# A router kernel on one core: spare matrix products while TensorE waits, a written-out first trip, an early table load, and one load fewer

## The chip, the cores and the metric

The kernel runs on one core of a Trainium2 chip. The metric is the device time in microseconds; the kernel before takes 85.81 us (median of three runs, 85.59 to 85.82). The profiled execution has a span of 84.4 us, from its first to its last instruction.

## The reference

```python
def setup_inputs():
    batch, seq, dim = 16, 512, 1024
    num_loras = 8
    return {
        "x": np.random.randn(batch, seq, dim).astype(np.float32),
        "router_weights": np.random.randn(dim, num_loras).astype(np.float32),
    }

def reference(x, router_weights):
    logits = np.matmul(x, router_weights)
    exp_logits = np.exp(logits - np.max(logits, axis=-1, keepdims=True))
    return (exp_logits / np.sum(exp_logits, axis=-1, keepdims=True)).astype(np.float32)
```

There are 8192 rows of x, each of 1024 numbers. Every row is multiplied by a 1024 x 8 matrix and a softmax is taken over the 8 results. The input x is 33.55 MB, the output 0.26 MB.

## The kernel before

Each of the 128 partitions holds 64 rows of x (the text calls them rows 0 to 63; one such "row" is 128 rows of the input, one a partition). Rows 0 to 3 are loaded as float32 from the Sync queue and cast by ScalarE. Rows 4 to 63 are loaded by GpSimd's queue, which turns float32 into bfloat16 on the way. TensorE transposes the eight 128 x 128 blocks of a row, VectorE copies five of them from PSUM to SBUF and ScalarE three, and TensorE multiplies the copies with the weights. Groups of eight rows then go through the softmax on VectorE and ScalarE.

```python
LOADS = [4] + [8] * 4 + [4] * 4 + [2, 2, 2] + [1] * 5   # rows in each load
PIECES = [4, 2, 2]                     # row 63 comes in three pieces of its columns
G, SKIP = 8, 4
TRIPS = 31
VN, SN = 5, 3                          # blocks copied by VectorE, by ScalarE
# ... (cut)
X_AT = place[0]
xa = sb("x_all", [P, J, D], bf16)      # all 64 rows have their own place: no load waits for a buffer
x_f32 = sb("x_f32", [P, LOADS[0], D], fp32)
# ... (cut)  Sync tells TensorE of rows as their loads land
for i, r in enumerate(LOADS):
    if i:
        sp.wait_ge(s_ld[i], 16)
        sp.sem_inc(s_in, r)
# ... (cut)  the loads, all issued at the start on one queue
for i, r in enumerate(LOADS):
    if i:
        nc.gpsimd.dma_start(
            out=xa[:, first[i]:first[i] + r, :], in_=x_rows[:, first[i]:first[i] + r, :]
        ).then_inc(s_ld[i], 16)
# ... (cut)
def loop_turn(b):                      # transposes one row; its address is in registers r_x
    pe.wait_ge(s_in, 1).then_inc(s_in, -1)
    for c in range(KO):
        t = again(turn_like, ...)      # eight transposes 128x128
    # ... (cut) registers go on by one row

def multiply(b, dst):
    for c in range(KO):
        if c == 0:
            pe.wait_ge(s_c[b], 2).then_inc(s_c[b], -2)
        m = ...                        # eight products 128x8

def fill():                            # a spare product; its result is never read
    return pe.matmul(spare, lhsT=filler[:, 0:P], rhs=filler, start=True, stop=True)
# ... (cut)
turn(0)
pe.wait_ge(s_wb, 1)
nc.br("rows_turn", engines=only_pe)
with nc.body("rows_multiply", valid_engines=only_pe):
    fill()
    fill()
    multiply(1, None)
    pe.br("rows_turn")
with nc.body("rows_turn", valid_engines=only_pe):
    loop_turn(1)
    multiply(0, None)
    loop_turn(0)
    pe.br_lt(r_x[0], left_of(TRIPS - 1), on_true="rows_multiply", on_false="rows_done")
nc.switch_bb("rows_done")
# ... (cut)  after the loop: row 63 by its pieces
pe.wait_ge(s_c[(J - 3) % 2], 2)
turn_piece(0)
multiply((J - 3) % 2, alone[1])
turn_piece(1)
turn_piece(2)
multiply((J - 2) % 2, alone[2])
# ... (cut)  ScalarE's start
act.wait_ge(s_f, 16).then_inc(s_f, -16)   # rows 0 to 3 have landed
for i in range(2):
    cast(i)
    for j in (2 * i, 2 * i + 1):
        act_copy(j, j)
```

Of the kernel before, what the change touches and what calls it, by code (L numbers as in the profile page):

```python
# [11 lines left out]
def kernel(  # L12
# [6 lines left out]
    nc = tc.nc  # L19
    P = 128  # L20
    B, S, D = x.shape
# [10 lines left out]
    fp32 = mybir.dt.float32  # L32
    bf16 = mybir.dt.bfloat16
    Exp = mybir.ActivationFunctionType.Exp
    X = mybir.AxisListType.X
    ALU = mybir.AluOpType

    LOADS = [4] + [8] * 4 + [4] * 4 + [2, 2, 2] + [1] * 5  # L40
    PIECES = [4, 2, 2]
    G, SKIP = 8, 4
    TRIPS = 31
# [5 lines left out]
    DONE = ends[-1]  # L49
    assert sum(LOADS) == J - 1 and sum(PIECES) == KO and ends[-1] == J - ALONE  # L50
    VN, SN = 5, 3

    place = [16640]

    def sb(name, shape, dtype):
        size = mybir.dt.size(dtype)
        for n in shape[1:]:
            size *= n
        at = place[0]
        place[0] = -(-(at + size) // 64) * 64  # L60
        return nc.alloc_sbuf_tensor_at(name, shape, dtype, offset=at).ap()
# [1 line left out]
    def ps(name, shape, dtype):  # L63
        return nc.alloc_psum_tensor(name, shape, dtype).ap()

    X_AT = place[0]
    xa = sb("x_all", [P, J, D], bf16)
    x_f32 = sb("x_f32", [P, LOADS[0], D], fp32)
    identity = sb("identity", [P, P], bf16)
    ident = sb("ident", [P, P], fp32)  # L70
    w8 = sb("w8", [KO, P, N], fp32)
# [31 lines left out]
    s_w = nc.alloc_semaphore("s_w")  # L103
    s_ld = [sem(f"s_ld{i}") for i in range(len(LOADS))]
    s_z = [sem(f"s_z{i}") for i in range(len(PIECES))]
# [21 lines left out]

    first = [sum(LOADS[:i]) for i in range(len(LOADS))]
    cols = [sum(PIECES[:i]) for i in range(len(PIECES))]


    with tc.manual_schedule():
        early = [
            nc.sync.dma_start(out=x_f32, in_=x_rows[:, 0:LOADS[0], :]).then_inc(s_f, 16),
            nc.scalar.dma_start(
# [25 lines left out]

    for j in range(LOADS[0]):
        sp.wait_ge(s_cast, j + 1)
# [34 lines left out]
    pe = nc.tensor  # L198
    r_x = [pe.alloc_register(f"rx{c}") for c in range(KO)]
    r_l = pe.alloc_register("rl")  # L200
    for c, r in enumerate(r_x):

        pe.reg_mov(r, X_AT + D * 2 + c * P * 2 + (P - 1) * 2)
    pe.reg_mov(r_l, LG_AT + 256 * (SKIP - 1))

    def at(ap, like, r):
        return mybir.RegisterAccessPattern(
            ap=ap, dtype=like.dtype, memsetref=like.tensor.name + "_set",
            regref=r.name, is_regloc_offset=False, reg_ap_offset=r.name,
            const_ap_offset=0, const_sub_tensor_id=0,  # L210
        )

    def again(like, **k):
        return pe.add_instruction(copy.replace(like, name=f"I-{nc.next_id()}", **k))

    def turn_ap(b, c):
        return (ptv if c < VN else pts)[b][:, c if c < VN else c - VN, :]

    def chunk(b, c):
        return xTv[b][:, c, :] if c < VN else xTs[b][:, c - VN, :]  # L220

    def loop_turn(b):

        pe.wait_ge(s_in, 1).then_inc(s_in, -1)  # L224
        for c in range(KO):
            t = again(
                turn_like,
                ins=(turn_like.ins[0], at([[J * D, P], [1, P]], xa, r_x[c])),
                outs=(pe.lower_ap(turn_ap(b, c), opt=False),),
            )  # L230
            if c == VN - 1:
                t.then_inc(s_tv, 1)
            if c == KO - 1:
                t.then_inc(s_ts, 1)
        pe.reg_add(r_l, r_l, 256)
        for c in range(KO):
            if c == KO // 2:
                pe.reg_alu(r_l, r_l, -4097, ALU.bitwise_and)
            pe.reg_add(r_x[c], r_x[c], D * 2)
# [10 lines left out]
# [5 lines that stand above are left out]
            if dst is None:  # L255
                m = again(
                    mult_like,
                    ins=(
                        pe.lower_ap(w_bf[:, c, :], opt=False),
                        pe.lower_ap(chunk(b, c), opt=False, for_matmul_weights=True),  # L260
                    ),
                    outs=(at([[2 * G * 64, P], [1, N]], lg, r_l),),
                    start_tensor_calc=(c == 0),
                    stop_tensor_calc=(c == KO - 1),
                )
            else:
                m = pe.matmul(  # L267
                    dst, lhsT=chunk(b, c), rhs=w_bf[:, c, :],
                    start=(c == 0), stop=(c == KO - 1),
                )  # L270
            if c == KO - 1:
                m.then_inc(s_p, 1)

    def fill():
        return pe.matmul(spare, lhsT=filler[:, 0:P], rhs=filler, start=True, stop=True)  # L275
# [17 lines left out]
    def left_of(i):  # L293

        return X_AT + D * 2 * (2 * i + 3) + (P - 1) * 2

    only_pe = OrderedEngineSet([pe.engine])
    nc.br("rows_turn", engines=only_pe)
    with nc.body("rows_multiply", valid_engines=only_pe):
        fill()  # L300
        fill()
        multiply(1, None)
        pe.br("rows_turn")
    with nc.body("rows_turn", valid_engines=only_pe):
        loop_turn(1)
        multiply(0, None)
        loop_turn(0)
        pe.br_lt(r_x[0], left_of(TRIPS - 1), on_true="rows_multiply", on_false="rows_done")
    nc.switch_bb("rows_done")


# [30 lines left out]
    act = nc.scalar  # L342
# [14 lines left out]
    def act_copy(j, seen):  # L357

        act.wait_ge(s_ts, seen + 1)
        act.copy(xTs[j % 2], pts[j % 2][:, 0:SN, :]).then_inc(s_c[j % 2], 1)  # L360

    act.wait_ge(s_f, 16).then_inc(s_f, -16)  # L362
    for i in range(2):
        cast(i)
# [181 lines left out]
```

## Time and profile before

| Quantity | Value |
|---|---|
| Time, median of 3 runs | 85.81 us (85.59 to 85.82) |
| Span of the profiled execution | 84.4 us |
| Busy: TensorE products, TensorE weight loads | 62.4 us (74%), 52.3 us (62%) |
| Busy: VectorE, ScalarE, GpSimd | 39.4 us (47%), 38.0 us (45%), 11.3 us (13%) |
| Transposes of rows (L288) | 311 of 226 ns and 186 of 228 ns, as recorded |
| Spare products (L275, 128x512) | 61, 402 ns each as recorded |
| Table load of ScalarE | 1, 1.28 us, at 8.50 us |
| Read from HBM | 33.59 MB |

The engines are PE (TensorE's products), PEld (its weight loads), DVE (VectorE), ACT (ScalarE), POOL (GpSimd) and SP (Sync). L288 means line 288 of the kernel. A matrix product's recorded duration overlaps the next one's, so the step from one start to the next is what the engine really spends. A wait is listed with the engine that waits, the one that ended it, the total, the count and the longest. "PEq" is TensorE's own sequencer: a wait that ends there is one that the sequencer sat through, for a semaphore that was raised elsewhere.

### The profile page before, as it was taken

How to read it: one execution, taken by the hardware profiler on the slowest of the kernel's cores; microseconds unless marked ns; L12 is line 12 of the kernel's file. 1: busy time of each engine (PE TensorE's matmuls, PEld its weight loads, DVE VectorE, ACT ScalarE, POOL GpSimd, SP SyncE). 2: the span in 40 equal slices, each digit the busy share in tenths (PEclk: the TensorE clock that was granted, in tenths of full speed). 3: DMA queues.
4: the chain of work that ended last, by engine and by line, in shares of the span. 5: the costliest groups of instructions: out<-in, count | busy, mean ns of one | idle time of the engine just before them, and what ended most of it. 6: DMA issues, size and time to landing. Idle time of an engine off the chain costs nothing. (4 is left out here: it accounts for less than half of the span.)

```text
span 84.4 us, 2916 instructions
## 1 busy us (share of the span) xinstructions
PE 62.4 (74%) x1094; PEld 52.3 (62%) x1094; DVE 39.4 (47%) x114; ACT 38.0 (45%) x81; POOL 11.3 (13%) x26
## 2 busy tenths in 40 slices
PE   0070073999991999259990999999998799999870
PEld 0040072788871778238870688887887588777650
DVE  0030022247660685227660265678568357656662
ACT  0000988535460465225460254566546246546470
POOL 0699996000000000000000000000000000000000
PEclk9999999999999999999998579999999999999997
DMA  5999979997999799989998999999999999999930
GB/s 142 433 419 264 225 163 233 241 217 171 241 241 217 163 248 233 202 186 248 233 202 179 225 210 217 217 206 225 206 229 190 214 212 215 204 207 213 171 114 12
DMA packets 3184, 18.12 MB, mean 215 GB/s; under 512 B 488, under 2 KB 1000, under 8 KB 2032
## 3 DMA queue, kind: packets, MB, share of 16 engines
q0 software_dynamic: 2736, 15.73, 90.3%
q1 hardware_dynamic: 432, 2.36, 7.3%
q10 hardware_dynamic: 16, 0.03, 0.2%
HBM read 33.59 MB, written 0.26 MB: 401 GB/s over the span
## 5 line engine op out<-in xcount | busy, mean ns | idle before, releaser
L405 DVE COPY xTv<-ptv 128x640 bf16<-128x640 bf16 x63 | 31.0, 492 | 32.9 <-PE ptv L288 26.7
L360 ACT COPY xTs<-pts 128x384 bf16<-128x384 bf16 x63 | 30.1, 477 | 34.0 <-PE pts L288 33.6
L288 PE MATMUL ptv<-identity,x_all 128*128 128x128 bf16 x311 | 29.0, 226 | 14.4 <-PEq L224 9.5
L288 PEld LDWEIGHTS ptv<-identity,x_all 128*128 (+1 forms) x311 | 19.0, 99 | 15.4 <-issue 15.4
L288 PE MATMUL pts<-identity,x_all 128*128 128x128 bf16 x186 | 21.7, 228 | 0.0
L275 PEld LDWEIGHTS lg<-w_bf,xTv 128*128 128x128 bf16 x305 | 15.7, 98 | 7.9 <-issue 1.3
L275 PE MATMUL spare<-filler 128*128 128x512 bf16 x61 | 19.6, 402 | 0.2
L275 PE MATMUL lg<-w_bf,xTv 128*128 128x8 bf16 x305 | 16.7, 167 | 0.0
L288 PEld LDWEIGHTS pts<-identity,x_all 128*128 x186 | 13.9, 103 | 0.0
L275 PE MATMUL lg<-w_bf,xTs 128*128 128x8 bf16 x183 | 13.2, 166 | 0.0
L275 PEld LDWEIGHTS lg<-w_bf,xTs 128*128 128x128 bf16 x183 | 9.0, 96 | 0.0
L180 POOL DMA_DIRECT2D x_all<-in_x_dram x16 | 8.6, 588 | 2.2 <-POOLq L142 2.2
L275 PEld LDWEIGHTS spare<-filler 128*128 128x128 bf16 x61 | 4.7, 103 | 1.1 <-issue 1.0
L346 ACT ACT_TABLE_LOAD x1 | 1.3, 1283 | 8.5 <-ACTq L362 8.5
L282 PE MATMUL lg<-ident,w 8*128 8x8 f32 x8 | 1.0, 251 | 4.7 <-PEq L280 4.7
L346 ACT CAST x_all<-x_f 128x1024 bf16<-128x1024 f32 x4 | 4.0, 1044 | 0.0
L425 DVE TENSOR_REDUCE mx<-lg 128x8 f32 x8 | 1.8, 225 | 4.6 <-DVEq L475 4.1
L282 PEld LDWEIGHTS lg<-ident,w 8*128 8x128 f32 x8 | 0.9, 197 | 4.7 <-issue 4.7
L349 ACT ACTIVATE ev<-ex 128x64 f32<-128x64 f32 x8 | 2.1, 257 | 1.5 <-DVE ex L425 0.9
L396 DVE CAST identity<-ident 128x128 bf16<-128x128 f32 x1 | 0.5, 518 | 4.6 <-POOL ident L186 4.6
L441 DVE TENSOR_REDUCE ssum<-ev 128x8 f32<-128x64 f32 x8 | 1.7, 218 | 0.1
L425 DVE TENSOR_TENSOR ex<-lg,mx 128x64 f32<-128x64 f32 x8 | 1.7, 216 | 0.0
(41 smaller groups left out, 16.0 us busy)
## 6 DMA issues: line engine op xcount, KB each, us to landing
x_all<-in_x_dram POOLq DMA_DIRECT2D x4, 2048.0 KB, 27.7
x_all<-in_x_dram POOLq DMA_DIRECT2D x4, 1024.0 KB, 51.7
x_f<-in_x_dram SPq DMA_DIRECT2D x1, 2048.0 KB, 8.4
x_all<-in_x_dram POOLq DMA_DIRECT2D x3, 512.0 KB, 62.0
x_all<-in_x_dram POOLq DMA_DIRECT2D x5, 256.0 KB, 66.2
out_dram<-out_all SPq DMA_DIRECT2D x1, 240.0 KB, 2.0
x_all<-in_x_dram POOLq DMA_DIRECT2D x1, 128.0 KB, 67.8
x_all<-in_x_dram POOLq DMA_DIRECT2D x2, 64.0 KB, 67.5
```

What stands on the lines that cost most here:

```text
L180: nc.gpsimd.dma_start(out=xa[:, first[i]:first[i] + r, :], in_=x_rows[:, first[i]:first[i] + r, :]).then_inc(s_ld[i], 16)
L275: return pe.matmul(spare, lhsT=filler[:, 0:P], rhs=filler, start=True, stop=True)
L282: t = pe.transpose(w_ps[:, n, :], w8[:, :, n], ident[0:KO, 0:KO])
L288: turn_like = pe.transpose(turn_ap(0, 0), xa[:, 0, 0:P], identity).ins
L346: act.copy(xa[:, k, :], x_f32[:, k, :]).then_inc(s_cast, 1)
L349: return act.activation(ev, ex, func=Exp).then_inc(s_ev, 1)
L360: act.copy(xTs[j % 2], pts[j % 2][:, 0:SN, :]).then_inc(s_c[j % 2], 1)
L396: dve.tensor_copy(out=identity, in_=ident).then_inc(s_idb, 1)
L405: dve.tensor_copy(out=xTv[j % 2], in_=ptv[j % 2][:, 0:VN, :]).then_inc(s_c[j % 2], 1)
L425: return dve.add_instruction(kind(name=f"I-{nc.next_id()}", engine=dve.engine, **k))
L441: dve.reduce_sum(ssum[:, :, 0], ev, axis=X).then_inc(s_d, 1)
```

## The change

There are four parts.

1. A block of six spare products is put ahead of TensorE's loop. The loop goes through it before the rows that open a new load of eight (and before row 36), so that TensorE has something to do while it waits. A test of the row's address decides; for that test x is moved in SBUF to byte 40,960 of a partition (20 rows of 2 KB), and the float32 buffer is put ahead of it.
2. The loop's first trip is written out, so that the loop begins with the spare products and the multiplication of an odd row.
3. ScalarE loads its table of functions before it waits for rows 0 to 3, and no longer after.
4. Rows 52 to 62 come in seven loads, 3, 2, 2, 1, 1, 1, 1, where there were eight, 2, 2, 2, 1, 1, 1, 1, 1.

```diff
-    LOADS = [4] + [8] * 4 + [4] * 4 + [2, 2, 2] + [1] * 5
+    LOADS = [4] + [8] * 4 + [4] * 4 + [3, 2, 2] + [1] * 4
@@
+    LOT, SPARE = 8, 6
+    ROW_AT = 32 - LOADS[0] - LOT
+    assert LOADS[1:5] == [LOT] * 4 and 64 - ROW_AT == LOADS[0] + LOT * 5
@@
-    X_AT = place[0]
+    x_f32 = sb("x_f32", [P, LOADS[0], D], fp32)
+    place[0] = X_AT = ROW_AT * D * 2
     xa = sb("x_all", [P, J, D], bf16)
-    x_f32 = sb("x_f32", [P, LOADS[0], D], fp32)
@@
+    r_t = pe.alloc_register("rt")
@@
-    nc.br("rows_turn", engines=only_pe)
-    with nc.body("rows_multiply", valid_engines=only_pe):
+
+    loop_turn(1)
+    multiply(0, None)
+    loop_turn(0)
+    nc.br("rows", engines=only_pe)
+    with nc.body("rows_spare", valid_engines=only_pe):
+        for _ in range(SPARE):
+            fill()
+        pe.br("rows_even")
+    with nc.body("rows", valid_engines=only_pe):
         fill()
         fill()
         multiply(1, None)
-        pe.br("rows_turn")
-    with nc.body("rows_turn", valid_engines=only_pe):
         loop_turn(1)
         multiply(0, None)
+        pe.reg_alu(r_t, r_x[0], (64 + 32 + LOT - 1) * D * 2, ALU.bitwise_and)
+        pe.br_eq(r_t, 32 * D * 2, on_true="rows_spare", on_false="rows_even")
+    with nc.body("rows_even", valid_engines=only_pe):
         loop_turn(0)
-        pe.br_lt(r_x[0], left_of(TRIPS - 1), on_true="rows_multiply", on_false="rows_done")
+        pe.br_lt(r_x[0], left_of(TRIPS - 1), on_true="rows", on_false="rows_done")
     nc.switch_bb("rows_done")
@@
+    act.preload_act_table(Exp)
     act.wait_ge(s_f, 16).then_inc(s_f, -16)
```

## The prediction

> **What bounds the kernel now.** I read the DMA lines of the page first, then the waits of the Sync queue, then TensorE's timeline around its waits, then the chain that ended last.
>
> ```profile
> DMA  5999979997999799989998999999999999999930
> q0 software_dynamic: 2736, 15.73, 90.3%
> HBM read 33.59 MB, written 0.26 MB: 401 GB/s over the span
> ```
>
> The DMA engines are busy from the second slice to the 38th, so to about 80 us. GpSimd's queue alone fills 90.3% of their span. The input's 33.55 MB pass through them once and nothing else of size does.
>
> ```profile
> SPq L168 <- DMA x_all<-in_x_dram: 63.6, 16, 9.7
> ```
>
> Sync tells TensorE of each landed load, and it sits idle for all 16 loads in turn, 9.7 us for one of eight rows: 8 x 0.524 MB = 4.19 MB in 9.7 us is 432 GB/s. That is the pace at which rows come: 1.21 us each.
>
> ```profile
> 43.92 0.22 PE L275 MATMUL lg<-w_bf,xTs 128*128 128x8 bf16 x3
> 46.55 0.69 PE L288 MATMUL ptv<-identity,x_all 128*128 128x128 bf16 x5 [2.41 <-PEq L224]
> 47.04 0.52 PE L288 MATMUL pts<-identity,x_all 128*128 128x128 bf16 x3
> 47.36 1.06 PE L275 MATMUL spare<-filler 128*128 128x512 bf16 x2
> ...
> 64.99 0.22 PE L275 MATMUL lg<-w_bf,xTs 128*128 128x8 bf16 x3
> 66.02 0.44 PE L288 MATMUL ptv<-identity,x_all 128*128 128x128 bf16 x5 [0.81 <-PEq L224]
> ```
>
> TensorE (start, recorded duration, idle before in brackets) finishes row 27, waits 2.41 us for the load of rows 28 to 35, and then runs at half speed: five transposes are recorded with 0.69 us, where they have 0.44 later. It is at full speed again from row 30 (49.53 us). In spite of that it has caught up at row 48, where it waits 0.81 us again for a load. At full speed two rows with their two spare products take 1.73 us (start of the spare pair at 22.00, of the next at 23.73), 0.86 us a row against the 1.21 us in which rows come.
>
> ```profile
> 79.66 0.44 PE ptv L288 x5
> 80.10 0.17 PE pts L288 x3
> 80.27 0.01 issue
> 80.28 0.38 PE pts L321 x4
> 80.66 0.18 PE spare L267 x8
> 80.85 0.13 PE ptv L321 x2
> 80.98 0.20 PE extra L321 x2
> 81.18 0.18 PE lg L267 x8
> ```
>
> The chain that ended last (start, duration, what) begins only at 79.66 us, with row 62. The trace's landing records put the last of row 62's load at 79.49 us, and row 63's pieces at 80.10, 80.46 and 80.85: TensorE takes each as it comes. From the last landing to the end of the span are 84.4 - 80.85 = 3.5 us of dependent small steps and the last store. So the time is the arrival of x plus that tail.
>
> **What the Trainium skill says.**
> - "TensorE: Matmul & The Clock Gate", section "Part 1: The HAM clock gate": TensorE's clock is halved after an idle window of about 3.4 us, windows run freely, and a busy window gives full speed back. The trace agrees: its clock records have one half-speed stretch inside the work, from 45.98 us for 3.41 us. The two earlier waits (1.99 us before row 12, 2.48 us before row 20) were followed by none, as a freely running window would have it.
> - "ScalarE: Activation LUTs", section "What ACT_TABLE_LOAD costs": about 1283 ns for a load. The trace has 1283 ns, at 8.50 us, right after rows 0 to 3 landed (8.40 us).
> - "DMA: Bandwidth & Descriptors", section "Bandwidth": 435 GB/s is the ceiling of the path into SBUF. The 432 GB/s above is at it, so the loads have no reserve.
> - "Runtime: NRT & Kernel Launch", section "Instruction fetch mechanics": a taken branch to code outside the two fetched pages stalls. In the trace all 13 packets of instruction fetch come before the first instruction, so the loop of before fetches nothing while it runs.
>
> **The change part by part.**
>
> *Six spare products.* Two spare products move the next start by 0.43 us (22.00 to 22.43), so six take 1.29 us. The address test, read off row by row, is true ahead of rows 12, 20, 28 and 36. Ahead of the first three they fall into waits of 1.99, 2.48 and 2.41 us and leave 0.7, 1.2 and 1.1 us of idle: no cost. With so little idle in a row the clock should stay up, which saves the slow rows 28 and 29: 46.55 to 49.53 is 2.98 us for the pair, 1.25 us more than 1.73. Ahead of row 36 TensorE is late (its load landed at 51.21 us, the row starts at 54.71) and the six cost their full 1.29 us. The two cancel: TensorE reaches row 36 at 46.55 + 4 x 1.73 + 1.29 = 54.76 us, against 54.71. On the path that sets the end: 0.
>
> *First trip written out.* The same instructions as the first trip of before, in the same order; one address operation and one compare are added to each of 31 trips, between products that TensorE has queued already. The loop had two branches a trip and has two still. 0.
>
> *Early table load.* It moves from 8.50 us to some 0.7 us, after ScalarE's own DMA issue (0.12 + 0.58 us), into an 8.5 us wait. The casts and rows 0 to 3 come 1.28 us earlier. Row 4 would then start at 17.61 - 1.28 = 16.3 us, but its load lands at 17.29 us by the landing records, so it starts at about 17.45 and 0.16 us are left of it. Row 12 waits for its load at 26.97 us in either case. On the path: 0.
>
> *One load fewer.* The landing records let the cost of a load be fitted. Four loads of four rows take 65.85 - 46.38 = 19.47 us, 4.87 each; three of two rows 73.25 - 65.85 = 7.40, 2.47 each; five of one row 79.49 - 73.25 = 6.25, 1.25 each. From the first and last: (4.87 - 1.25) / 3 = 1.206 us a row and 1.25 - 1.21 = 0.04 us a load; for two rows this gives 2.46, measured 2.47. Rows 52 to 62 in seven loads thus arrive at 65.85 + 11 x 1.206 + 7 x 0.044 = 79.42 us, some 0.05 us earlier than now. This lies on the path, and row 63's pieces follow behind it. What it may give back: row 52 now lands with row 54, at 65.85 + 3.66 = 69.51, not at 68.26. TensorE came to row 52 at 69.68 us, and a landed load reaches it in some 0.17 us (65.85 to 66.02), so it just meets it.
>
> *Sum.* 0 + 0 + 0 - 0.05 us on the path: 85.81 - 0.05 = 85.76. I say 85.7, as the third time of before is 85.59 and its median stands at the upper edge of their range.
>
> **The rivals.**
>
> *TensorE's speed decides, and the warm clock is a gain.* If the lost 1.25 us at rows 28 to 31 came through to the end, the time would be about 84.5. For it: TensorE's products are busy 74%, and the half-speed stretch is real. Against it: the waits of 0.81 us at row 48 and 0.41 us at row 62, both after the stretch. A delay that is followed by a wait for data is gone.
>
> *The spare products cost at row 36.* If no slow stretch came in most executions of before, the change would make TensorE 1.29 us later there. But from row 36 to row 48 it gains 12 x (1.21 - 0.86) = 4.2 us on the loads, and row 36 started 3.5 us late. Even 1.29 us later still, it would be 0.6 us late at row 48, and the next rows take that back. This leaves 85.7; only a much slower loop would let it through, to 86 or 87.
>
> *The loads bound it whatever is done ahead of them.* This is what I hold: 85.7.
>
> *Fetching of instructions.* TensorE's program grows by 24 matrix products and six spare ones, with a weight load for each, and its loop is now three blocks. If the loop or the exit from it crossed into a page that isn't there, each crossing would stall TensorE. No run here shows how long that takes; late in the kernel it would add its whole length, and 85.7 + 1.8 = 87.5 is what it would have to reach for a verdict of slower. Against it: no such fetch in the trace before, and the code is still short.
>
> *Fewer, larger loads delay the last rows.* Row 52 comes 1.25 us later, and with it nothing to do for TensorE if it is early. Rows 59 to 62 still come one by one, at the times of now. So nothing of it reaches the end.
>
> **Range and chances.** The times of before spread by 0.23 us, and the known change on the path is 0.05 us, less than that. I take 85.4 to 86.0 us as the range that holds it 8 times in 10: the central 85.7 with some 0.3 us to each side, for a change of the arrival by a little or a tail that shifts. Faster by over 2% would need less than 84.1 us, which is less than even the first rival gives: 0.02. Slower by over 2% means over 87.5, only with stalls of fetching: 0.02. Within 2%: 0.96.
>
> **What would show each step right or wrong.** In the profile of the changed kernel I expect the last piece of x to land at 80.8 us, as now, and the last chain to begin at row 62 again, near 79.6. Six spare products should stand ahead of rows 12, 20, 28 and 36, the first three with a wait of about 1 us behind them, and the slow pairs near 47 us should be gone. The table load should stand near 0.7 us and the first cast near 8.5, and row 4 should wait for its load. The waits of TensorE late in the kernel should still be there, at row 48 or at the rows after it. I am wrong if the loads land at another pace, if TensorE comes to row 62 without a wait, or if TensorE idles where no load is awaited.

## The result and the profile after

The changed kernel takes 86.83 us (median of six runs, 86.61 to 87.21), the kernel before 85.62 us beside it: the ratio is 1.0137, with a 95% interval of 1.011 to 1.0163. It is 1.2 us slower.

| Quantity | Before | After |
|---|---|---|
| Time, median | 85.62 us | 86.83 us |
| Span of the profiled execution | 84.4 us | 84.8 us (84.7 to 84.8 in all six runs) |
| Time less span, median of all runs | 1.3 us | 2.0 us |
| Last piece of x lands | 80.85 us | 80.57 us |
| TensorE's trip of two rows where no load is awaited, 54 to 79 us | 1.73 us | 1.88 us |
| Instructions of TensorE in the built program, weight loads included | 204 | 275 |

The 65 runs of the kernel before that stand beside e1 to e11 have a median span of 84.3 us, and their time is 1.27 to 1.37 us above it. So about 0.5 us of the loss lies within the span, and about 0.7 us outside it. The profile's page of after, with the granted clock and the DMA engines:

```profile
PEclk9999999999999999999999999999999999999999
DMA  5999969997999799979996999999999999999920
```

By the clock's records it is at full speed from 20.42 us on (before: from 18.67) and doesn't fall again before the end of the span; the nines ahead of that are no record, as five transposes at 17.28 us still take 0.69 us. The DMA engines are as full as before. The spare products do what they were meant to do for the clock. Now the waits, first of before, then of after (who waited for what: total, count, longest):

```profile
PE ptv L288 <- PEq L224: 9.5, 6, 2.5
PEld spare L275 <- issue: 1.0, 5, 0.2
```

```profile
PEld spare L283 <- issue: 4.6, 25, 0.4
PE ptv L296 <- PEq L232: 2.9, 4, 1.4
```

TensorE's waits for rows fell from 9.5 to 2.9 us. In their place stands a small gap ahead of the spare products of nearly every trip, 25 times, with no other engine to blame ("issue"). After's timeline of TensorE (start, recorded duration) shows the last wait for a load, the block ahead of row 36, and the gap:

```profile
46.38 0.54 PE L296 MATMUL ptv<-identity,x_all 128*128 128x128 bf16 x5 [0.34 <-PEq L232]
...
54.25 1.45 PE L283 MATMUL spare<-filler 128*128 128x512 bf16 x6
55.54 0.44 PE L296 MATMUL ptv<-identity,x_all 128*128 128x128 bf16 x5
...
65.44 0.61 PE L283 MATMUL spare<-filler 128*128 128x512 bf16 x2
...
67.32 0.61 PE L283 MATMUL spare<-filler 128*128 128x512 bf16 x2
```

From 46.38 us to the end of the loop TensorE waits for no load again; before, it waited at row 48 and at row 62. From one pair of spare products to the next are now 67.32 - 65.44 = 1.88 us. The chain that ended last says the same: it no longer begins at 79.66 us with row 62, but at row 28. Its last part (start, duration, what):

```profile
78.16 0.30 PE ptv L296 x5
78.45 0.17 PE pts L296 x3
78.62 0.59 PE spare L283 x2
79.21 0.20 PE lg L283 x8
79.40 0.02 issue
79.43 0.24 DVE mx L443
...
80.83 0.37 ACT xTs L377
81.19 0.50 ACT xTz L407
81.69 0.14 issue
81.83 0.35 PE lg L352 x8
```

Row 62 has landed at 79.28 us, but TensorE turns it at 79.89; the spare pair at 78.62 and the softmax steps that then bunch up on VectorE and ScalarE stand ahead of the last products, which come at 81.83 us and not at 81.43.

The rest of the 1.2 us is not in the span. The DMA records of after hold one packet of instruction fetch that before has not: 16,384 bytes, on queue 8, from 86.07 us for 1.01 us, when the span has ended at 84.82.

My theory A had two halves: in the loop, TensorE's sequencer (which issues, waits, branches and counts registers) needs longer for a trip than the products do, and with the six products at row 36 this makes TensorE late at the end; after it, a fetch of instructions comes because TensorE's program has grown. Theory B was that the slower loop is all of it, and theory C that the first trip, the loads or the table load cost it. The limit of 256 instructions that some expectations name is the length of a fetched block by the page that "Why the prediction was wrong" cites; e5 and e9 test it.

### The profile page after: what moved, and what is told of

It is laid out like the page before. It is cut to its first block, busy times and chain, and to the rows that moved or that the text cites. A ratio compares the mean times of both kernels' runs of the same rounds, so it can differ in the third digit from the quotient of the medians.

```text
span 84.8 us, 3025 instructions
## 1 busy us (share of the span) xinstructions
PE 70.0 (83%) x1118; PEld 53.6 (63%) x1118; DVE 39.3 (46%) x114; ACT 37.9 (45%) x81; POOL 10.8 (13%) x25
## 5 line engine op out<-in xcount | busy, mean ns | idle before, releaser
L283 PE MATMUL spare<-filler 128*128 128x512 bf16 x85 | 25.5, 396 | 0.7 <-issue 0.5
L283 PEld LDWEIGHTS spare<-filler 128*128 128x128 bf16 x85 | 5.8, 99 | 6.7 <-issue 4.6
L187 POOL DMA_DIRECT2D x_all<-in_x_dram x15 | 8.1, 586 | 2.2 <-POOLq L149 2.2
```

The costliest lines, as they stand in the source:

```text
L187: nc.gpsimd.dma_start(out=xa[:, first[i]:first[i] + r, :], in_=x_rows[:, first[i]:first[i] + r, :]).then_inc(s_ld[i], 16)
```

## The experiments

Each ratio is against the kernel before, run beside it on the same chip.

### Without the block and the test (e1)

```diff
-    with nc.body("rows_spare", valid_engines=only_pe):
-        for _ in range(SPARE):
-            fill()
-        pe.br("rows_even")
...
-        pe.reg_alu(r_t, r_x[0], (64 + 32 + LOT - 1) * D * 2, ALU.bitwise_and)
-        pe.br_eq(r_t, 32 * D * 2, on_true="rows_spare", on_false="rows_even")
-    with nc.body("rows_even", valid_engines=only_pe):
```

> The changed kernel without the spare block and without the address test in the loop; written-out trip, early table load and seven loads stay. Theory A (the span's extra 0.4 us comes from the test's time in TensorE's sequencer and the six products at row 36; the other 0.8 us from an instruction fetch after the last instruction, which comes once TensorE's program is over 256 instructions): trip back to 1.73 us, row 62 waits for its load again, span 84.2 to 84.4. By the count of the built program TensorE has 260 instructions (275 in the changed kernel, 204 before), so the fetch may stay: 86.2 with it, 85.5 without. Theory B (all of the 1.2 us is the slower loop): 85.5. Theory C (the written-out trip, the loads or the table load cost it): 86.8 stays.

Measured: 86.08 us against 85.70, ratio 1.0045 (1.0028 to 1.0062). The trip is back to 1.73 us where it doesn't wait, and TensorE waits for rows again. The span is 84.9, not 84.2 to 84.4: here the fetch comes at 82.56 us, before the end and not after it, and the last store lands at 84.85 us; the table-and-loads version (e4, below) issues it at 82.90 us too and has it landed at 84.32 us. The test's part of theory A holds; the fetch has a second form that I had not expected.

### Code that is never run (e2, e5, e9)

```diff
-    nc.br("rows_turn", engines=only_pe)
+    pe.br_eq(r_x[0], 0, on_true="rows_never", on_false="rows_turn")
+    with nc.body("rows_never", valid_engines=only_pe):
+        for _ in range(36):          # e5: 24, e9: 12
+            fill()
+        pe.br("rows_turn")
```

> The kernel before, with a block of 36 spare products ahead of the loop that is never entered; TensorE's program has 277 instructions and runs what it ran before, plus one compare at the start. Theory A: span as before, 84.4; a fetch of 16 KB after the last instruction; time up by 0.8 us, to 86.4. Theory B (the fetch is harmless, all is the loop): 85.6, as before.

Measured for e2: 86.77 us against 85.70, ratio 1.0124 (1.0108 to 1.0141), with a span of 84.5. Code that is never entered costs 1.07 us where theory A gave 0.8, nearly all of it outside the span. The fetch of 16 KB is there, at 85.81 us. Theory B falls.

> The kernel before with a block of 24 spare products that is never entered: TensorE's built program has 253 instructions, where the block of 36 made 277. Theory A (a fetch after the end comes when the program passes 256 instructions): no fetch, 85.7. If it is the mere presence of the block or the compare ahead of the loop: 86.7 as with 36. If the limit lies lower, as other code is fetched with it: a fetch, and up to 86.7.

Measured for e5: 86.00 us against 85.62, ratio 1.0052 (1.0024 to 1.008), single runs from 85.70 to 86.84. The profiled execution is one of the longest, 86.76 us with a span of 85.4. The fetch is there too, at 82.79 us.

> The kernel before with a block of 12 spare products that is never entered: 229 instructions in TensorE's built program (253 and 277 in the two runs with larger blocks). If only the length of the program counts and the limit lies between 229 and 253: no fetch, span 84.4, time 85.6 to 85.7. If the block or the compare ahead of the loop costs by itself: 86 or more.

Measured for e9: 86.14 us against 85.54, ratio 1.0064 (1.0043 to 1.0085), span 84.9, fetch at 81.94 us. So the limit isn't at 256 of the built program's instructions, where I had put it, nor between 229 and 253. Without a program between 204 and 229 that has the block, e9 alone leaves open that the block or the compare costs. But e3 (below), with 219 instructions, two blocks more than before and a compare, has no fetch.

All runs by the length of TensorE's program, with what their DMA records show. The span is that of the profiled execution; the last two columns are medians over all runs of a kernel. The lengths of e8, e10 and e11 follow from their edits (e10 and e11 have two products with their weight loads fewer).

```
kernel                  instructions  16 KB fetch at  span ends  time, median  time less span
e10 large, no spare          200           none         85.52        86.99          1.3
e11 no spare                 200           none         84.05        85.52          1.3
before                       204           none         84.42        85.62          1.3
e4 table and loads           204           none         84.36        85.71          1.3
e8 large loads               204           none         86.50        87.78          1.3
e3 no first trip             219           none         84.48        85.65          1.3
e9 never run, 12             229         81.94 us       84.89        86.14          1.3
e5 never run, 24             253         82.79 us       85.43        86.00          1.3
e1 no test                   260         82.56 us       84.89        86.08          1.3
after                        275         86.07 us       84.82        86.83          2.0
e6 spare off                 275         85.58 us       84.32        86.46          2.1
e7 one more                  276         88.16 us       86.80        89.02          2.4
e2 never run, 36             277         85.81 us       84.53        86.77          2.3
```

No program of up to 219 instructions has the fetch, every one from 229 on has it. In the middle lengths it falls among the output stores and costs 0.4 to 0.6 us: in e9 the fetch is one packet of 1.42 us, and eight of the first store's 128 packets, which take 76 to 81 ns otherwise, begin only at 83.36 us, as the fetch ends, and take up to 211 ns; that store has fully landed at 84.67 us, and before at 82.82. In the longest it starts 1.2 to 1.4 us after the span's end, and the time less span is 2.0 to 2.4 us instead of 1.3: some 0.7 to 1.0 us that no span shows. The runs don't separate the length of the program from the place that the code behind the added part takes.

### The first trip not written out (e3)

```diff
-    loop_turn(1)
-    multiply(0, None)
-    loop_turn(0)
-    nc.br("rows", engines=only_pe)
+    nc.br("rows_odd", engines=only_pe)
...
         multiply(1, None)
+        pe.br("rows_odd")
+    with nc.body("rows_odd", valid_engines=only_pe):
         loop_turn(1)
```

> The changed kernel with its loop entered in the middle, as before, instead of the first trip written out: spare block and test stay, TensorE has 219 instructions. Theory A: no fetch after the end, trip of 1.88 us or slightly more (one more branch), span 84.8 to 85.0, time 86.0 to 86.2, so 0.7 to 0.8 us under the changed kernel. Theory B: 86.8 as the changed kernel, or more. Theory C with the written-out trip as its cause: span falls to 84.4 and time to 85.6.

Measured: 85.65 us against 85.70, ratio 0.9997 (0.9983 to 1.0011), span 84.5. There is no fetch, as theory A has it, but the span is shorter than it expected, and the time is the 85.6 that theory C gave for the written-out trip as the cause. The trip is 1.83 us, not 1.88 or more, and that is enough for TensorE to have caught up when row 62 comes. TensorE's timeline of e3:

```profile
78.08 0.60 PE L283 MATMUL spare<-filler 128*128 128x512 bf16 x2
79.71 0.44 PE L296 MATMUL ptv<-identity,x_all 128*128 128x128 bf16 x5 [0.20 <-PEq L232]
```

It waits 0.20 us for row 62 (landed at 79.54). So the written-out trip costs in two ways: by its 24 products, with a weight load each, it takes the program over the limit, and a trip takes 0.05 us more with it. Why the second is so stays open. The move of x in SBUF, which no run tests alone, is in e3 and costs nothing there.

### Early table load and seven loads alone (e4)

```diff
-    LOADS = [4] + [8] * 4 + [4] * 4 + [2, 2, 2] + [1] * 5
+    LOADS = [4] + [8] * 4 + [4] * 4 + [3, 2, 2] + [1] * 4
...
+    act.preload_act_table(Exp)
```

> The kernel before with the early table load and the seven loads alone. Theory A and B: the arrival of x bounds it, the last piece lands 0.05 to 0.3 us earlier, time 85.3 to 85.6. Theory C with these two as its cause: 86 or more.

Measured: 85.71 us against 85.70, ratio 0.999 (0.9971 to 1.0009). These two parts do nothing to the time; theory C has no support from them.

### The block never entered (e6)

```diff
-        pe.br_eq(r_t, 32 * D * 2, on_true="rows_spare", on_false="rows_even")
+        pe.br_eq(r_t, 33 * D * 2, on_true="rows_spare", on_false="rows_even")
```

> The changed kernel with a value in the address test that never comes: test and block stay (275 instructions), the 24 spare products of the block are not run. Theory A: trips stay at 1.88 us, but TensorE is 1.29 us earlier from row 36 on and waits for row 62 (46.4 + 17 x 1.88 = 78.3, row 62 lands near 79.4); span 84.3 to 84.4, the fetch stays, time 86.3 to 86.5. If the slower trip alone set the span: 84.8 and 86.8 stay.

Measured: 86.46 us against 85.62, ratio 1.0089 (1.0057 to 1.0121), span 84.3. The trips are 1.88 us, and the span is that of the kernel before; the 24 spare products are 0.5 us of the changed kernel's span. The slow trip alone doesn't reach the end, and e3, with the six products at row 36 and a trip of 1.83 us, doesn't either. Nearly the whole of this kernel's loss of 0.84 us is outside the span, with the fetch at 85.58 us. Its timeline shows that the waits, which the spare products filled, are back:

```profile
36.73 0.44 PE L296 MATMUL ptv<-identity,x_all 128*128 128x128 bf16 x5 [1.94 <-PEq L232]
46.39 0.44 PE L296 MATMUL ptv<-identity,x_all 128*128 128x128 bf16 x5 [1.85 <-PEq L232]
```

### One more instruction of the sequencer (e7)

```diff
         multiply(0, None)
+        pe.sem_inc(s_n, 1)
         pe.reg_alu(r_t, r_x[0], (64 + 32 + LOT - 1) * D * 2, ALU.bitwise_and)
```

> The changed kernel with one more instruction of the sequencer in each trip, an increment of a semaphore that nobody waits for. Theory A (TensorE's sequencer, not its products, sets the trip of 1.88 us): trip 1.97 to 2.03 us, 17 trips from row 28 to row 62 make 1.5 to 2.6 us: span 86.3 to 87.4, time 88.4 to 89.4. Rival (the products or the copies of the other engines set the trip): trip 1.88 as before, time 86.8.

Measured: 89.02 us against 85.62, ratio 1.04 (1.0358 to 1.0442), span 86.8. The spare products of three trips in a row (this trace has one record for each pair):

```profile
62.52 0.39 PE L284 MATMUL spare<-filler 128*128 128x512 bf16 x1
64.55 0.39 PE L284 MATMUL spare<-filler 128*128 128x512 bf16 x1
66.53 0.39 PE L284 MATMUL spare<-filler 128*128 128x512 bf16 x1
```

The trips are 2.03 and 1.98 us. An instruction that moves no data and that nobody waits for lengthens each trip by 0.10 to 0.15 us and the kernel by 2.2 us. The sequencer sets the trip, as theory A has it.

### Larger loads (e8), and without the spare products in the trips (e10, e11)

These look for a version that beats both.

```diff
-    LOADS = [4] + [8] * 4 + [4] * 4 + [2, 2, 2] + [1] * 5
+    LOADS = [4] + [8] * 6 + [3, 2, 2] + [1] * 4     # e8 and e10; e11 has e4's loads
...
-        fill()      # e10 and e11
-        fill()
         multiply(1, None)
```

All three have the early table load.

> A version that may beat both: the kernel before with the early table load and with rows 4 to 51 in six loads of eight, rows 52 to 62 in seven: 13 loads where there were 16. At 0.04 us a load the last piece lands some 0.1 us earlier than in the kernel before: 85.5 to 85.6 if the arrival of x sets the end and TensorE, which gets rows 36 to 51 in larger lots, is not made late; 85.7 if the cost of a load is hidden; over 86 if the larger lots make TensorE late.

Measured: 87.78 us against 85.62, ratio 1.0242 (1.0205 to 1.0278), span 86.5. The third of the three outcomes came: TensorE is late. TensorE in e8:

```profile
65.80 0.44 PE L288 MATMUL ptv<-identity,x_all 128*128 128x128 bf16 x5 [1.30 <-PEq L224]
...
80.26 0.59 PE L275 MATMUL spare<-filler 128*128 128x512 bf16 x2
82.27 0.40 PE L321 MATMUL pts<-identity,x_all 128*128 128x128 bf16 x4
```

It gets rows 44 to 51 at once at 65.80 us, needs 0.86 us a row, and comes to row 63 at 82.27 us, 1.5 us after its last piece (80.78). The last piece came no earlier than in e4 (80.72), so nothing was won for it.

> The version with 13 loads, which was slower, without the two spare products in each trip. A trip then takes 1.73 - 0.43 = 1.30 us at full clock, and 2.98 - 0.85 = 2.13 us at half, both under the 2.42 us in which two rows arrive. If TensorE's lateness after the large lots was what made 13 loads slower: it catches up by row 57, span about 84.3, time 85.5 to 85.7. If the spare products are needed for the clock at the end: 86.0 to 86.6, with a half clock in the last 10 us.

Measured: 86.99 us against 85.54, ratio 1.0171 (1.0152 to 1.0189), span 85.5. A miss by both readings: the clock is full in the last 10 us, and still TensorE is late. The clock line of e10, and its transposes of rows 56 and 58:

```profile
PEclk9999999999999659999996557956999579999999
```

```profile
75.86 0.44 PE L288 MATMUL ptv<-identity,x_all 128*128 128x128 bf16 x5
...
77.44 0.44 PE L288 MATMUL ptv<-identity,x_all 128*128 128x128 bf16 x5
```

The clock's records have four halved stretches again, from 28.45, 45.51 (6.83 us long), 55.75 and 65.99 us, and at full clock a trip is 77.44 - 75.86 = 1.58 us, not the 1.30 that the products need. Here too the products don't set it.

> The kernel before with early table load and seven loads (85.71 in its own run) without the two spare products in each trip. If the arrival of x alone sets the end: 85.6 to 85.8, as with them. If the clock falls at the end without them: the last row's steps on TensorE take about half as long again, some 0.3 to 0.6 us more: 86.0 to 86.3.

Measured: 85.52 us against 85.54, ratio 1.0002 (0.9991 to 1.0014). The clock and the waits of e11:

```profile
PEclk9999999999998589975999659999999956999999
```

```profile
PE ptv L288 <- PEq L224: 13.1, 9, 2.5
```

The clock is halved four times and TensorE waits 13.1 us for rows, and the time is that of before. With these loads the spare products of the trips are worth nothing either. No version here beats the kernel before.

## Why the prediction was wrong

It said 85.7 us, with 85.4 to 86.0, and measured is 86.83. The bound was read rightly: the arrival of x and its tail set the time before, and gains ahead of it are lost. Two steps failed, both on what the change adds. Two of the prediction's own signs of being wrong came: TensorE comes to row 62 without a wait, and it idles where no load is awaited, in the 25 gaps ahead of the spare products. One reading of the bound was loose: 432 GB/s counts the float32 bytes that are read. Into SBUF go half as many, 216 GB/s, so the ceiling of the path into SBUF isn't what these loads reach. What is full is the DMA engines: a packet of 16,384 bytes takes 1.23 us on the queue that converts, and 0.61 us on the one that doesn't.

**"First trip written out … 0", with the test counted in it.** The step said that the added address operation and compare lie "between products that TensorE has queued already", and that the loop has two branches a trip as before. It counted instructions, not the sequencer's time, and it counted the branches wrongly: the trace of before has one branch a trip (the jump to the block that stands next leaves no record), that of after two. The records of TensorE's sequencer, start to start, for one trip of each, in us (where the sequencer of before has to wait, at the ends of the second and the last line, after's figure stands):

```
                                        before     after
wait for copies, wait for row, odd       0.302     0.302
registers and on to the next wait        0.338     0.338
wait for copies, even                    0.151     0.150
test: address operation                    -       0.093
test: compare, not taken                   -       0.133
wait for row, even                       0.151     0.236
registers and on to the loop's compare   0.333     0.343
loop's compare, taken, to the next wait  0.285     0.285
sum                                      1.56      1.88
```

Before, 1.56 us lay hidden under 1.73 us of products: 0.17 us of reserve. The test takes 0.23 us, and a wait for a row has 0.085 us more that I can't explain. In e3 this wait takes 0.150 us (at 75.45 and 77.28 us), which is where its trip is shorter. At 1.88 us the sequencer sets the trip, as e7 shows by adding to it, and e10 by taking products away: 1.58 us are left there, close to the 1.56 of the sum. In the profile the test is small. The loop's one branch of before, then the two instructions of after's test (durations in ns as least, median, most; first and last start):

```profile
L308 PEldq COMPARE_BRANCH  x31: 76/208/232, 15.0 to 80.0; - x31
```

```profile
L321 PEldq ALU_OP  x30: 32/32/32, 15.3 to 79.4; - x30
```

```profile
L322 PEldq COMPARE_BRANCH  x30: 75/75/207, 15.4 to 79.5; - x30
```

The test's 32 and 75 ns are the recorded durations; from start to start the two hold 226 ns. The Trainium skill, "Advanced Engine Details and Errata", section "Control Flow Timing", gives about 108 ns for a compare-and-branch; here it is 133 ns from start to start where it isn't taken, and 285 where it is (266 in e10, with no spare products behind it).

**The spare products.** The three first blocks fell into waits, at no cost, and the clock stayed up: right, and worth nothing, as e4 (clock halved from 37.56 us for 3.41 us) and e11 show with the same time. The waits left behind them were 0, 0.42 and 0.34 us, not 0.7, 1.2 and 1.1, as TensorE was later there already (trips of 1.88 us, and full clock only from 20.42 us). (The clock of before changes at 18.67, 45.98 and 49.39 us, whole multiples of 3.41 us apart. The window of that length ahead of the halving, from 42.57 us, had products in it up to 44.14 us: it was not idle throughout, though the prediction calls it an idle window and says that the trace agrees.) Ahead of row 36 the block cost its 1.29 us (54.25 to 55.54), right. "The two cancel … On the path that sets the end: 0" was wrong twice. From row 28 to row 36, block and all, TensorE took 55.54 - 46.38 = 9.16 us where 54.76 - 46.55 = 8.21 were counted, and the lateness was then to be caught up at 0.86 us a row. At 0.94 it catches up 12 x (1.21 - 0.94) = 3.2 us by row 48 where 4.2 were counted. From 55.54 us 26 rows end at 55.54 + 26 x 0.94 = 79.98; row 62 is turned at 79.89 us, 0.6 us after its load. The rival of the six products, of which the prediction says that "only a much slower loop would let it through", was the right one for the span, and the loop need be slower only by 0.15 us in 1.73. The slow trip alone doesn't do it (e6: 84.3 us), nor the block with a trip of 1.83 us (e3: 84.5); no run has the block with a trip of 1.73 us.

**"Fetching of instructions … the code is still short."** This rival was put aside by looking at the loop, and its size was left open. It is the larger part. What I looked for was a fetch inside the loop or at its exit, and none comes there. It comes after the last instruction, and not for what the code does: e2 loses 1.07 us by code that never runs. "Runtime: NRT & Kernel Launch", section "Instruction fetch mechanics", of the Trainium skill says that instructions are fetched in blocks of 16 KB, 256 instructions. The packet's 16,384 bytes agree; the limit, between 219 and 229 instructions of the built program, lies below 256. Perhaps something is fetched with them that the program's own count doesn't have, or the count is another; no run here tells these apart. Also open: why the fetch comes near 82 us in programs of 229 to 260 instructions and after the end in longer ones.

**Early table load.** It costs and brings nothing, right. It stands at 2.16 us and not at 0.7, as ScalarE first sits through line 149, where every engine has semaphore records between 1.3 and 2.1 us:

```profile
2.16 1.28 ACT L379 ACT_TABLE_LOAD   x1 [2.16 <-PEq L149]
...
8.60 1.99 ACT L363 CAST x_all<-x_f 128x1024 bf16<-128x1024 f32 x2 [5.15 <-ACTq L380]
...
17.28 0.69 PE L296 MATMUL ptv<-identity,x_all 128*128 128x128 bf16 x5 [0.73 <-PEq L232]
```

Casts begin 1.2 us earlier and row 4 waits 0.73 us for its load, as foreseen.

**One load fewer.** Right to the size: from row 51's landing to row 62's are 79.49 - 65.85 = 13.64 us before and 79.28 - 65.68 = 13.60 after, 13.60 in e4 too: 0.04 us for a load. In e4 it can't be seen in the time.

The sum thus lacked two terms: about 0.5 us in the span (row 36's block on a trip of 1.88 us) and about 0.7 us behind it (the fetch). Together they are the 1.2 us.

## What to carry to other kernels

In a hand-made loop of small matrix products, count what TensorE's sequencer needs for a trip (waits, register operations, branches, start to start in the trace) beside what the products need: the reserve may be a tenth, and a test of two cheap instructions uses it up. Code that is never run can cost too: keep an eye on the count of an engine's instructions, look in the DMA records for a fetch that wasn't there, and compare the time with the span, since a loss outside the span is in no view of the engines. A wait that the bounding stream hides, and a clock that falls in it, are worth nothing to fill, as long as TensorE has caught up when the last data come (in e10 it had not).

## What the runs showed of the hardware that I had not expected

- A block of 36 products that is never entered costs 1.07 us, with one fetch of 16,384 bytes that starts 1.3 us after the last instruction.
- Where that fetch falls among output stores, eight of the 128 packets of a store of 240 KB begin only as its packet of 0.9 to 1.4 us ends (e9: at 83.36 us, e5: at 83.70), and the store lands up to 2.4 us later (e5: 85.22 us, before: 82.82).
- One semaphore increment of TensorE's sequencer, in a loop that it bounds, costs 0.10 to 0.15 us a trip, where its own record shows 51 ns.
